# Block products of two units interleaved, four plain units first, half of the output projection plain

## The chip, the cores and the metric

The kernel runs on one core of a Trainium2 chip. The metric is device time in microseconds (us) of one execution, the median of three runs. Beside it stands one profiled execution, whose trace gives every duration below.

## What is computed

One layer of a decoder trunk for 512 tokens of width 2048, all in float32. The input is normalised, one matrix of 2048 x 8192 maps it to eight groups of 1024 columns (q, f, i, g of a gated linear recurrence with 8 heads; q, k, v, g of a dilated ALiBi attention with 16 heads), both mixers run, and one matrix of 2048 x 2048 maps their joined outputs back onto the residual stream:

```python
h = rms_norm(x, norm_gain[layer])
z = jnp.einsum('bsd,de->bse', h, w_in[layer])
q_h, f_h, i_h, g_h, q_a, k_a, v_a, g_a = jnp.split(z, split_points, axis=-1)
y_h = hgrn2_mixer(q_h, f_h, i_h, lb_all[layer], hgrn_gnorm[layer]) * silu(g_h)
y_a = dilated_attention_mixer(q_a, k_a, v_a) * silu(g_a)
y = jnp.concatenate([y_h, y_a], axis=-1)
x = x + jnp.einsum('bse,ed->bsd', y, w_out[layer])
return rms_norm(x, final_gain)
```

## The kernel before, in words

**Pieces.** A float32 product is made from three fast products: each operand is cut into a high part, which ACT makes by a cast (`cut`, L107), and a low part, which DVE makes by subtracting (L108). Each pair of tiles then costs three matmuls: hi x hi, hi x lo, lo x hi. A cut weight piece is 128 x 512, and five pairs hi/lo are in flight (`piece`).

**Units.** The input projection is worked off in 32 units of 256 columns (two blocks of 128): 16 for the recurrent heads (two per head), 16 for the attention pairs (two per pair). `plain_unit` makes the first two units (PLAIN = 2) the usual way: 16 k tiles, two blocks, two halves of the tokens, three matmuls of 128x256 each, 192 in all.

**Seven products.** All other units use the Winograd form of Strassen's scheme: seven products of half size instead of eight, 168 matmuls. The sums of the input are made once: x7 in unit 0 (`x7`, L162), x5 and x6 in unit 1, x3 after it. The sums of weights are made while loading: a raw tile is loaded by an SP queue transfer (`begin`), and a transfer on POOL's queue adds the next block to it in place (`grow`, accumulating). Tile A is loaded once and grown three times (for products 7, 6, 4), B is loaded and grown once (1, 5), D and C are loaded (2, 3). In SBUF A has two tiles, B one, and C and D share one (`W_BUFS`, L567). The order within a unit is 7, 1, 2, 6, 3, 5, 4 (`ORDER`, L55). Each product has two steps; at each step `cut_w` cuts the pieces four steps ahead, and once a tile is cut for the last time in its present state it issues the next `begin` or `grow`.

**Banks.** Products 1, 6 and 5 accumulate in one PSUM bank (a), 7 and 4 in one of two (c), 2 and 3 open a third (t). After product 1, ACT copies the bank (L709), and only then may product 6 go on adding into it; so too after product 6 (L713) and product 5.

**Mixers.** Their work is put into a calendar of slots (`at_slot`, `tick`): one slot per step, whose functions are written ahead of that step's matmuls. The recurrent head begins with `work_f` and `work_q` at the end of its first unit and `work_v`, `work_g` at the end of its second; an attention pair with `work_aq`, `work_ak`, then `work_av`, `work_ag`. Finished outputs go to DRAM (`y_dram`).

**Output projection.** It is done in two halves of 1024 columns (u = 0, 1), each by seven products of 8 k tiles, two row blocks and three matmuls of 128x512 (`o_product`), 336 matmuls a half. Its left operand, y and the sums of y's blocks, is staged back from DRAM and cut: `y_71` during the last unit, `y_2653` and `y_4` in slots of the projection's first products. Raw weights come by `o_begin`/`o_grow`, cuts by `o_cut`, five pieces ahead. `evacuate` adds each product into the residual tiles, `squares` and `finish` do the last norm. `open_out2` loads the final gain and multiplies it into the first half's tiles on GpSimd (`gained`, L876).

Of the kernel before, what the change touches and what calls it, by code (L numbers as in the profile page):

```python
# [33 lines left out]
def _units():  # L34
    out = []
    for h in range(HEADS_H):
        out.append((("f", h, 1024 + P * h), ("q", h, P * h)))
        out.append((("v", h, 2048 + P * h), ("g", h, 3072 + P * h)))
    for j in range(PAIRS):
        out.append((("aq", j, 4096 + P * j), ("ak", j, 5120 + P * j)))  # L40
        out.append((("av", j, 6144 + P * j), ("ag", j, 7168 + P * j)))
    return out
# [3 lines left out]
PLAIN = 2  # L46
# [13 lines left out]
NEXT = {("A", 7): 6, ("A", 6): 4, ("B", 1): 5}  # L60
# [3 lines left out]
def tile_kernel(ctx: ExitStack, tc: tile.TileContext, x, xT, w_in, w_out, gain, lbl, gnorm, fgain,  # L64
# [45 lines left out]
    def x_tiles(m):  # L110

        return [tuple(xp.tile([P, 4, HS], F32R, tag=f"X{m}{p}{t}", name=f"X{m}{p}{t}") for p in "hl")
                for t in range(2)]
# [15 lines left out]
    def load_x(upto):  # L129
        while len(xts) < min(upto, KT):  # L130
            k = len(xts)
            xt = st.tile([P, S], F32, tag="xt", name=f"xt_{k}", bufs=9)
            nc.sync.dma_start(xt, xT[k * P:(k + 1) * P, :])
            xts.append(xt)
# [19 lines left out]
    def square_x(k):  # L154
        if k == 0:
            A.activation(acc, xts[k], AF.Square)
        else:
            sq = st.tile([P, S], F32, tag="sq", name=f"xsq_{k}", bufs=3)
# [181 lines left out]
    def work_q(h, q):  # L340
        V.scalar_tensor_tensor(q, q, 0.5, cs["rrow"], op0=ALU.mult, op1=ALU.mult)
        H[h]["q"] = q
        at_slot(2, silu, q, H["hg"], "t", 1, f"q{h}")

    def work_g(h, g):
        V.scalar_tensor_tensor(g, g, 0.5, cs["rrow"], op0=ALU.mult, op1=ALU.mult)
        H[h]["g"] = g
        at_slot(3, silu, g, H["hg"], "t", 1, f"g{h}")

    def work_v(h, src):  # L350
        hg, aux, o = H["hg"], H[h], {}
# [90 lines left out]

    def work_aq(j, q):
        V.scalar_tensor_tensor(q, q, -0.125, cs["rrow"], op0=ALU.mult, op1=ALU.mult)
        H["aq"] = q

    def work_ak(j, k):
        V.tensor_mul(k, k, cs["rrow"])
        q = H["aq"]
# [26 lines left out]
        def scores(i, qb):  # L476
# [6 lines left out]
            p = pr[i, qb] = at.tile([P, S], F32, tag="pr", name=f"pr_{n}", bufs=4)  # L483
# [27 lines left out]

        d = H["wait"] = 4 if j == 0 else 0
        at_slot(d + 1, bias, 0)
        at_slot(d + 1, parts, 0)
        at_slot(d + 2, parts, 1)
        for n in range(8):
            at_slot(d + 4 + 2 * n, scores, n // 4, n % 4)
            at_slot(d + 4 + 2 * n + 3, turn, n // 4, n % 4)
        at_slot(d + 11, bias, 1)

    def work_ag(j, g):
        V.scalar_tensor_tensor(g, g, 0.5, cs["rrow"], op0=ALU.mult, op1=ALU.mult)
        H["pair", j]["g"] = g
        at_slot(2 + H["wait"], lambda: silu(g, H["at"], "pr", 4, f"ag{j}"))

    def work_av(j, src):
# [19 lines left out]
        at_slot(9 + H["wait"], values)  # L546
# [20 lines left out]
    W_BUFS = {"A": 2, "B": 1, "C": 1}  # L567
# [11 lines left out]
    def plain_weights(u):  # L579

        r = {}
        for n, (blk, tag) in enumerate(((W11, "A"), (W12, "B"), (W21, "A"), (W22, "C"))):
# [27 lines left out]
    def plain_unit(u):  # L610
# [3 lines left out]
        for k in range(KT):  # L614
            kg, kb = divmod(k, 4)
            t = kg % 2
            if u == 0:
# [18 lines left out]
            if kb == 2 and kg == 3 and u + 1 < PLAIN:  # L636
                cut_plain(u + 1, 0)
# [9 lines left out]
        if u == 0:  # L647
# [3 lines left out]
            close(st_cm)  # L651
            open_hg()
        for n, (kind, i, _) in enumerate(blocks):
# [3 lines left out]
            WORK[kind](i, z)  # L657


    steps = [(u, s, t) for u in range(PLAIN, len(UNITS)) for s in range(7) for t in range(2)]  # L660
    cuts = []

    def cut_w(upto):
        while len(cuts) < min(upto, len(steps)):
            u, s, t = steps[len(cuts)]
            m, b, _, _ = ORDER[s]
# [3 lines left out]
            if t == 1:  # L670
                if m == 2:
                    begin(u, "C")
                if (b, m) in NEXT:
                    grow(u, b, NEXT[b, m])
                elif u + 1 < len(UNITS) and b == "B":
                    begin(u + 1, "B")
                if u + 1 < len(UNITS):
                    if m == 3:
                        begin(u + 1, "D")
                    if m == 6:  # L680
                        begin(u + 1, "A")
                        grow(u + 1, "A", 7)
# [3 lines left out]
    def product(u, s, i0):  # L686

        m, b, tag, opens = ORDER[s]
        if opens:
            banks[tag] = bank(tag, f"{tag}{m}_{u}")  # L690
        ps = banks[tag][:, :HS]
        for t in range(2):
# [4 lines left out]
            for kb in range(4):  # L697
# [4 lines left out]
                T.matmul(ps, lo[:, c], xh[:, kb], start=False, stop=en, skip_group_check=not opens)  # L702
        (k0, i, _), (k1, _, _) = UNITS[u]
# [12 lines left out]
        elif m == 5:  # L716
            for c in (slice(HS, S), slice(0, HS)):
                V.scalar_tensor_tensor(z["z1"][:, c], ps, -1.0, z["z1"][:, c], op0=ALU.mult, op1=ALU.subtract)
        else:
            V.tensor_add(z["z0"][:, HS:], ps, z["z0"][:, HS:])  # L720
            for n, (kind, _, _) in enumerate(UNITS[u]):
                WORK[kind](i, z[f"z{n}"])
# [4 lines left out]
    Y = {}  # L727

    def staged(k, tag, pool, bufs):
        s = pool.tile([P, S], F32, tag=tag, name=f"ys_{k}_{now[0]}", bufs=bufs)  # L730
# [7 lines left out]
    def y_cut(m, kb, src):  # L738
        cut(*y_parts(m, kb), src)

    def y_71(kb):
        for m in (7, 1):
            if m not in Y:
                Y[m] = x_tiles(m)
        h = staged(kb, "zA", zp, 2)
        V.tensor_sub(h[:, HS:], h[:, :HS], h[:, HS:])
        y_cut(7, kb, h[:, HS:])
        y_cut(1, kb, h[:, :HS])

    def y_2653(kb):  # L750

        for m in (2, 6, 3, 5):
# [312 lines left out]
```

## Time and profile before

| what | value |
|---|---|
| median of three runs | 1075.66 us (1072.43 to 1079.53) |
| profiled execution | 1074.24 us |
| its span, first to last instruction | 1072.5 us |
| TensorE busy, mean granted clock | 954.5 us (89%), 0.959 |
| DVE busy | 768.2 us (72%) |
| ACT busy | 584.6 us (55%) |
| POOL busy | 245.5 us (23%) |

PE is TensorE, DVE VectorE, ACT ScalarE, POOL GpSimd, SP the engine whose queue issues most transfers. Busy time of PE counts overlapping matmuls once, and its idle time is what is left of a stretch. The granted clock is 1 at 2.4 GHz and 0.5 at 1.2 GHz.

### The profile page before, as it was taken

What the parts mean: (1) busy time and instruction counts of PE and PEld (TensorE: products, weight loads), DVE (VectorE), ACT (ScalarE), POOL (GpSimd) and SP (SyncE); (2) the same over time, 40 slices, a digit from 0 to 9 for tenths busy, and PEclk for the clock granted to TensorE, in tenths of its full rate; (3) what the DMA queues carried; (4) which work ended last, traced back from release to release, by engine and by line L of the source; (5) the groups of instructions that cost most, each with busy time, mean ns of one, the idle gap of its engine ahead of it and who ended that gap; (6) DMA issues with size and microseconds to landing.
All of it is one profiled execution on the core that took longest, in us unless ns stands there. A gap on an engine that the chain in (4) does not pass through costs nothing.

```text
span 1072.5 us, 18864 instructions
## 1 busy us (share of the span) xinstructions
PE 954.5 (89%) x7000; PEld 889.5 (83%) x7000; DVE 768.2 (72%) x1536; ACT 584.6 (55%) x1250; POOL 245.5 (23%) x259
## 2 busy tenths in 40 slices
PE   5768989899999999899999999999999686898795
PEld 4667889899989999899999899989898654677684
DVE  7899667675858576677877686867767677465756
ACT  6643645464545555466666565656666464354345
POOL 3512121222312121212232222222222210202500
PEclk9899999999999999999999999999999888989898
DMA  7225877777777777777777777777787989969644
GB/s 260 61 59 118 173 172 192 172 178 168 167 172 179 175 181 187 171 189 175 182 176 184 167 158 171 179 176 173 166 182 194 251 219 320 265 171 224 178 109 158
DMA packets 59581, 191.70 MB, mean 179 GB/s; under 512 B 6688, under 2 KB 6720, under 8 KB 59488
## 3 DMA queue, kind: packets, MB, share of 16 engines
q0 software_dynamic: 22624, 81.95, 42.8%
q1 hardware_dynamic: 36576, 108.02, 29.9%
q8 instruction: 55, 0.90, 0.3%
q10 hardware_dynamic: 288, 0.52, 0.1%
q14 instruction: 38, 0.31, 0.1%
HBM read 182.08 MB, written 8.39 MB: 178 GB/s over the span
## 4 chain that ended last, share of the span: by engine, by line
PE 37%; DMA 27%; DVE 19%; ACT 9%; issue 6%; POOL 1%; SPq 0%; ACTq 0%; DVEq 0%; POOLq 0%
DMA wA<-w_in_dram 11%; DMA wC<-w_in_dram 7%; DVE lo L108 5%; PE a L700 4%; PE a L701 3%; PE a L702 3%; ACT hi L107 2%; PE t L700 2%; PE t L702 2%; PE t L701 2%; PE ao L539 2%; DMA wB<-w_in_dram 2%; DMA r<-x_dram 2%; DMA ys<-yd 2%; PE oa L954 2%
## 5 line engine op out<-in xcount | busy, mean ns | idle before, releaser
L108 DVE TENSOR_TENSOR lo<-wA,hi 128x512 fp32r<-128x512 f32 x180 | 127.7, 712 | 106.9 <-ACT hi L107 101.7
L107 ACT CAST hi<-wA 128x512 fp32r<-128x512 f32 x180 | 109.7, 618 | 147.0 <-DMA wA<-w_in_dram 78.1
L576 POOL DMA_DIRECT2D wA<-w_in_dram x90 | 79.2, 932 | 429.6 <-DVE lo L108 297.6
L107 ACT CAST hi<-wB 128x512 fp32r<-128x512 f32 x120 | 73.0, 618 | 43.2 <-PE a L701 20.2
L700 PE MATMUL a<-X6h,hi 128*128 128x256 f32 x240 | 73.1, 305 | 20.2 <-ACT f L709 15.7
L108 DVE TENSOR_TENSOR lo<-wB,hi 128x512 fp32r<-128x512 f32 x120 | 86.0, 730 | 0.3
L108 DVE TENSOR_TENSOR lo<-wC,hi 128x512 fp32r<-128x512 f32 x60 | 45.0, 770 | 56.2 <-ACT hi L107 55.8
L700 PE MATMUL a<-X5h,hi 128*128 128x256 f32 x240 | 70.0, 292 | 4.5 <-ACT v L713 4.2
L700 PE MATMUL t<-X3h,hi 128*128 128x256 f32 x240 | 70.1, 292 | 3.1 <-DVE v L711 1.5
L107 ACT CAST hi<-wC 128x512 fp32r<-128x512 f32 x60 | 35.7, 617 | 64.4 <-DMA wC<-w_in_dram 62.2
L700 PE MATMUL t<-X2h,hi 128*128 128x256 f32 x240 | 70.7, 295 | 0.0
L702 PE MATMUL a<-X6h,lo 128*128 128x256 f32 x240 | 70.6, 294 | 0.0
L701 PE MATMUL a<-X6l,hi 128*128 128x256 f32 x240 | 70.6, 294 | 0.0
L700 PE MATMUL a<-X1h,hi 128*128 128x256 f32 x240 | 70.4, 293 | 0.0
L702 PE MATMUL c<-X7h,lo 128*128 128x256 f32 x240 | 68.1, 284 | 2.1 <-DVE lo L108 2.1
L700 PE MATMUL c<-X4h,hi 128*128 128x256 f32 x240 | 68.9, 287 | 0.0
L701 PE MATMUL a<-X1l,hi 128*128 128x256 f32 x240 | 68.6, 286 | 0.0
L700 PE MATMUL c<-X7h,hi 128*128 128x256 f32 x240 | 68.6, 286 | 0.0
L702 PE MATMUL a<-X1h,lo 128*128 128x256 f32 x240 | 68.5, 285 | 0.0
L702 PE MATMUL t<-X2h,lo 128*128 128x256 f32 x240 | 68.3, 285 | 0.0
L701 PE MATMUL t<-X2l,hi 128*128 128x256 f32 x240 | 68.3, 284 | 0.0
L702 PE MATMUL t<-X3h,lo 128*128 128x256 f32 x240 | 67.9, 283 | 0.2 <-DVE lo L108 0.2
(369 smaller groups left out, 3452.4 us busy)
## 6 DMA issues: line engine op xcount, KB each, us to landing
wA<-w_in_dram POOLq DMA_DIRECT2D x90, 512.0 KB, 5.8
wA<-w_in_dram SPq DMA_DIRECT2D x30, 512.0 KB, 3.9
wB<-w_in_dram SPq DMA_DIRECT2D x30, 512.0 KB, 4.4
wD<-w_in_dram SPq DMA_DIRECT2D x30, 512.0 KB, 3.7
wB<-w_in_dram POOLq DMA_DIRECT2D x30, 512.0 KB, 8.6
wC<-w_in_dram SPq DMA_DIRECT2D x30, 512.0 KB, 5.8
oA<-w_out_dram POOLq DMA_DIRECT2D x24, 512.0 KB, 8.4
ys<-yd SPq DMA_DIRECT2D x32, 256.0 KB, 5.4
```

What stands on the lines that cost most here:

```text
L107: A.copy(hi, src)
L108: V.tensor_sub(lo, src, hi.bitcast(F32))
L539: T.matmul(o_ps[64 * i:64 * i + 64, kb * P:], pair["v"][:, kb, 64 * i:64 * i + 64], pt[:, c0:c0 + w], start=kb == 0, stop=kb == 3)
L576: nc.gpsimd.dma_start(raws[u, b], in_tile(u, GROW[b, m]), accum_op=ALU.add)
L700: T.matmul(ps, hi[:, c], xh[:, kb], start=st_, stop=False, skip_group_check=not opens)
L701: T.matmul(ps, hi[:, c], xl[:, kb], start=False, stop=False, skip_group_check=not opens)
L702: T.matmul(ps, lo[:, c], xh[:, kb], start=False, stop=en, skip_group_check=not opens)
L954: T.matmul(ps, xh[:, tok], lo, start=False, stop=en, skip_group_check=not opens)
```

## The change

Four units are plain (PLAIN = 4), and x7 is made in unit 1, x5 and x6 in units 1 and 2. The first head's g and v are made in unit 0, before its q and f. In the other units the blocks are exchanged (z1, the block that is ready after product 5, is now the one needed first), and product 4 is done after product 7 of the next unit. W11 is no longer read a second time for product 6: DVE adds the loaded tile B to A (`add_w11`). C and D have two tiles. The last two cuts of a plain unit are followed by the first two of the products (`cut_w(2)`).

The first half of the output projection (columns 0 to 1023) is made plainly by `o_plain`: y's two halves (kh: recurrent, attention), two column blocks, 8 k tiles, four row blocks, three matmuls of 128x512, 384 in all. Its y pieces are cut by `y_hgrn` (during the last unit) and `y_attn`; `y_sums` makes the sums for the seven products of the other half in slots of the plain half.

```diff
-PLAIN = 2
+PLAIN = 4
-ORDER = [(7, "A", "c", True), (1, "B", "a", True), (2, "D", "t", True), (6, "A", "a", False),
-         (3, "C", "t", True), (5, "B", "a", False), (4, "A", "c", False)]
+PRODUCT = {7: ("A", "c", True), 1: ("B", "a", True), 2: ("D", "t", True), 6: ("A", "a", False),
+           3: ("C", "t", True), 5: ("B", "a", False), 4: ("A", "c", False)}
-GROW = {("A", 7): W22, ("A", 6): W11, ("A", 4): W21, ("B", 5): W12}
+GROW = {("A", 7): W22, ("A", 4): W21, ("B", 5): W12}
...
-            p = pr[i, qb] = at.tile([P, S], F32, tag="pr", name=f"pr_{n}", bufs=4)
+            p = pr[i, qb] = at.tile([P, S], F32, tag="pr", name=f"pr_{n}", bufs=3)
...
-    W_BUFS = {"A": 2, "B": 1, "C": 1}
+    W_BUFS = {"A": 2, "B": 1, "C": 2}
...
-                    if i < KH:
-                        x7(i)
...
+                else:
+                    cut_w(2)
...
+    order = []
+    for u in range(PLAIN, len(UNITS) + 1):
+        for m in (1, 7, 2, 6, 3, 5) if u == PLAIN else (7, -4, 1, 2, 6, 3, 5):
+            v = u - 1 if m < 0 else u
+            if PLAIN <= v < len(UNITS):
+                order.append((v, abs(m)))
+    def add_w11(raw_a, raw_b):
+        for t in range(2):
+            c = slice(512 * t, 512 * t + 512)
+            V.tensor_add(raw_a[:, c], raw_a[:, c], raw_b[:, c])
...
+            if m == (7 if u == PLAIN else 1):
+                add_w11(raws[u, "A"], raws[u, "B"])
+                grow(u, "B", 5)
+                begin(u, "C")
+            elif m == 6:
+                grow(u, "A", 4)
+            if u + 1 < len(UNITS):
+                if m == 5:
                     begin(u + 1, "B")
+                elif m == 2:
+                    begin(u + 1, "D")
+            if m == 4 and u + 2 < len(UNITS) or u == PLAIN and m == 7:
+                v = u + 1 if m == 7 else u + 2
+                begin(v, "A")
+                grow(v, "A", 7)
...
+    def y_sums(kb):
+
+        y_tiles((7, 3), (5, 5), (6, 6), (3, 7))
+        h, a = staged(kb, O["w2"], "yh"), staged(KH + kb, O["w2"], "ya")
         a11, a21, a12, a22 = h[:, :HS], h[:, HS:], a[:, :HS], a[:, HS:]
+        V.tensor_sub(a11, a11, a21)
+        cut(*y_parts(7, kb), a11)
         V.tensor_sub(a21, a22, a21)
+        V.scalar_tensor_tensor(a22, a11, -1.0, a22, op0=ALU.mult, op1=ALU.subtract)
+        cut(*y_parts(6, kb), a22)
+        V.scalar_tensor_tensor(a12, a12, -1.0, a22, op0=ALU.mult, op1=ALU.subtract)
+        cut(*y_parts(3, kb), a12)
+        cut(*y_parts(5, kb), a21)
...
+    def o_plain(kh, n, i0):
+
+        tags = ("a", "c", "c", "t")
+        ob = [mixer_bank(f"op_{sb}") if kh and n else bank(tags[sb], f"op_{kh}_{n}_{sb}") for sb in range(NSB)]
+        for kb in range(KH):
+            for sb, ps in enumerate(ob):
+                if sb % 2 == 0:
+                    tick()
+                if sb == 1:
+                    o_cut(i0 + kb + 4)
+                hi, lo = ocuts[i0 + kb]
+                xh, xl = y_parts(((1, 21), (2, 4))[kh][sb // 2], kb)
+                tok = slice(sb % 2 * P, sb % 2 * P + P)
+                T.matmul(ps, xh[:, tok], hi, start=kb == 0, stop=False)
+                T.matmul(ps, xl[:, tok], hi, start=False, stop=False)
+                T.matmul(ps, xh[:, tok], lo, start=False, stop=kb == KH - 1)
+        for sb, ps in enumerate(ob):
+            r = O["R"][0, sb // 2, n, sb % 2]
+            V.tensor_add(r, ps, r)
+            if kh:
+                squares(0, sb // 2, n, sb % 2)
...
     at_slot(12, open_out)
+    for kb in range(KH):
+        at_slot(14 + 2 * kb, y_attn, kb)
+        at_slot(32 + 3 * kb, y_sums, kb)
+        if kb < 4:
+            at_slot(30 + 2 * kb, o_begin, "A", kb)
+            at_slot(31 + 2 * kb, o_begin, "B", kb)
+            at_slot(31 + 2 * kb, o_grow, "A", 7, kb)
```

## Rows read from the trace of the kernel before

**Rows 1.** The page, busy tenths of PE in 40 equal slices.
```profile
PE   5768989899999999899999999999999686898795
```

**Rows 2.** Busy time by stage: stretch, its length, PE, PEld, DVE, ACT, POOL, clock, DMA.
```profile
0.00:50.00 50.00, 30.69 (x189) 28.09 (x190) 40.18 (x69) 32.22 (x70) 24.79 (x25) 0.93 0.52 171
50.00:87.50 37.50, 28.65 (x216) 27.36 (x215) 34.22 (x57) 14.53 (x24) 6.17 (x8) 0.91 0.30 75
87.50:143.50 56.00, 49.08 (x390) 46.61 (x390) 44.60 (x82) 28.01 (x55) 10.67 (x13) 0.97 0.67 153
143.50:442.50 299.00, 278.11 (x2348) 273.67 (x2348) 210.60 (x427) 155.06 (x318) 66.25 (x72) 0.98 0.75 175
442.50:848.00 405.50, 390.29 (x3157) 374.78 (x3156) 297.59 (x639) 251.33 (x568) 98.10 (x100) 0.99 0.78 179
848.00:1062.00 214.00, 177.67 (x711) 139.03 (x709) 136.21 (x253) 100.02 (x210) 38.47 (x41) 0.90 0.78 209
1062.00:1072.50 10.50, 0.00 (x0) 0.00 (x0) 4.80 (x13) 3.39 (x6) 1.10 (x2) 0.59 0.53 201
```

**Rows 3.** Timeline of PE around one stall: start, duration, instruction, idle before.
```profile
353.45 0.28 PE L701 MATMUL t<-X2l,hi 128*128 128x256 f32 x1
353.57 0.28 PE L702 MATMUL t<-X2h,lo 128*128 128x256 f32 x1
356.10 0.39 PE L700 MATMUL a<-X6h,hi 128*128 128x256 f32 x1 [2.25 <-ACT f L709]
...
357.83 0.41 PE L700 MATMUL a<-X6h,hi 128*128 128x256 f32 x1
```

**Rows 4.** Timeline of ACT around the same stall.
```profile
355.16 0.62 ACT L107 CAST hi<-wC 128x512 fp32r<-128x512 f32 x1 [4.29 <-DMA wC<-w_in_dram]
355.68 0.37 ACT L709 COPY f<-a 128x256 f32<-128x256 f32 x1
```

**Rows 5.** Waits of PE, 143.5 to 442.5: total, times, longest.
```profile
PE a L700 <- ACT f L709: 15.2, 6, 3.2
PE a L700 <- ACT v L713: 4.2, 5, 1.7
```

**Rows 6.** Waits of ACT, 143.5 to 442.5.
```profile
ACT hi L107 <- DMA wC<-w_in_dram: 35.5, 12, 5.1
ACT hi L107 <- DMA wA<-w_in_dram: 34.7, 11, 4.5
```

**Rows 7.** Waits of PE in the output projection, 848 to 1062.
```profile
PE ot L952 <- ACT hi_o L107: 11.8, 2, 7.0
PE ot L954 <- DVE lo_o L108: 9.6, 4, 6.0
PE oc L952 <- DVE av L720: 5.5, 1, 5.5
```

**Rows 8.** Groups of DVE in unit 0: busy us, mean ns of one, idle before.
```profile
L168 DVE SCALAR_TENSOR_TENSOR X7l<-d,gain_sb,X7h 128x256 fp32r<-128x256 f32 x8 | 4.8, 605 | 0.0
```

**Rows 9.** Timeline of DVE in unit 0.
```profile
35.52 0.47 DVE L152 SCALAR_TENSOR_TENSOR X2l<-xt,gain_sb,X2h 128x256 fp32r<-128x256 f32 x1
35.91 0.47 DVE L152 SCALAR_TENSOR_TENSOR X4l<-xt,gain_sb,X4h 128x256 fp32r<-128x256 f32 x1
36.31 1.50 DVE L152 SCALAR_TENSOR_TENSOR X2l<-xt,gain_sb,X2h 128x256 fp32r<-128x256 f32 x1
```

**Rows 10.** Groups of DVE in the second plain unit (one sum of x5).
```profile
L178 DVE TENSOR_TENSOR d<-X4h,X3h 128x1024 f32<-128x1024 f32 x2 | 2.4, 1209 | 0.6 <-PE rrow_ps L262 0.6
```

**Rows 11.** Timeline of PE in the output projection.
```profile
971.06 0.39 PE L954 MATMUL oc<-lo_o,X7h 128*128 128x512 f32 x1
971.29 0.39 PE L952 MATMUL oc<-hi_o,X7h 128*128 128x512 f32 x1
```

**Rows 12.** The page, DMA issues: engine, count, KB each, median us to landing.
```profile
wB<-w_in_dram POOLq DMA_DIRECT2D x30, 512.0 KB, 8.6
wC<-w_in_dram SPq DMA_DIRECT2D x30, 512.0 KB, 5.8
...
ys<-yd SPq DMA_DIRECT2D x32, 256.0 KB, 5.4
```

**Rows 13.** Timeline of DVE after the final gain has landed.
```profile
1001.62 12.05 DVE L108 TENSOR_TENSOR lo_o<-oD,hi_o 128x512 fp32r<-128x512 f32 x4 [2.89 <-ACT hi_o L107]
```

More of the change, by code (lines that the diff above doesn't have):

```diff
@@ L108, in cut, with x_tiles @@
         V.tensor_sub(lo, src, hi.bitcast(F32))
-    def x_tiles(m):
-        return [tuple(xp.tile([P, 4, HS], F32R, tag=f"X{m}{p}{t}", name=f"X{m}{p}{t}") for p in "hl")
+    def x_tiles(m, of=None):
+        return [tuple(xp.tile([P, 4, HS], F32R, tag=f"X{of or m}{p}{t}", name=f"X{m}{p}{t}") for p in "hl")
                 for t in range(2)]
@@ L718, in product, with staged @@
                 V.scalar_tensor_tensor(z["z1"][:, c], ps, -1.0, z["z1"][:, c], op0=ALU.mult, op1=ALU.subtract)
+            WORK[k1](i, z["z1"])
         else:
             V.tensor_add(z["z0"][:, HS:], ps, z["z0"][:, HS:])
-            for n, (kind, _, _) in enumerate(UNITS[u]):
-                WORK[kind](i, z[f"z{n}"])
+            if u == 2 * HEADS_H:
+                close(H["cm"])
+                close(H["dcm"])
+                open_at()
+            WORK[k0](i, z["z0"])
     Y = {}
-    def staged(k, tag, pool, bufs):
-        s = pool.tile([P, S], F32, tag=tag, name=f"ys_{k}_{now[0]}", bufs=bufs)
+    O = {}
+    def staged(k, pool, tag):
+        s = pool.tile([P, S], F32, tag=tag, name=f"ys_{k}_{now[0]}", bufs=2)
         nc.sync.dma_start(s, y_dram[k])
@@ L736, in y_parts, with y_tiles @@
         return tuple(a[:, b] for a in Y[m][t])
[L738 to L742, printed above, removed]
+    def y_tiles(*which):
+        for m, of in which:
             if m not in Y:
[L744 to L752, printed above, removed]
-            if m not in Y:
-                Y[m] = x_tiles(m)
-        h, a = staged(kb, "zB", zp, 2), staged(KH + kb, "zA", zp, 2)
+                Y[m] = x_tiles(m, of)
@@ L838, in open_out @@
         O["ssq"] = w2.tile([P, NSB, 4], F32, name="ssq")
-        for jb in range(2):
-            o_begin(0, "D", jb)
         O["R"] = {}
@@ L848, in open_out @@
                     O["R"][0, th, n, blk] = r
-        for fn in O.pop("late"):
-            fn()
-        O["late"] = None
     def open_out1():
         for i, (th, n) in enumerate(((1, 1), (0, 0), (1, 0), (0, 1))):
-            r = xp.tile([P, 2, 512], F32, tag=("X7h0", "X7l0", "X7h1", "X7l1")[i], name=f"r1_{th}_{n}")
+            r = xp.tile([P, 2, 512], F32, tag=("X3h0", "X3l0", "X3h1", "X3l1")[i], name=f"r1_{th}_{n}")
             for blk in range(2):
@@ L868, in open_out2 @@
             O["fg"].append(f)
-        O["sq"] = xp.tile([P, 2, 512], F32, tag="X1l0", name="osq")
-        for key in O["R"]:
-            if key[0] == 0:
-                gained(*key)
-    def gained(u, th, n, blk):
-        r = O["R"][u, th, n, blk]
-        G.tensor_mul(r, r, O["fg"][u][:, 512 * n:512 * n + 512])
+        for u, th, n, blk in O["R"]:
+            if u == 0:
+                r = O["R"][u, th, n, blk]
+                G.tensor_mul(r, r, O["fg"][0][:, 512 * n:512 * n + 512])
     def squares(u, th, n, blk):
```

296 lines of the change are left out of this document (142 added, 154 removed).

## The prediction

> **What bounds the kernel now.** I read the page's slices first: TensorE is at 98% or more in the middle and clearly lower in about the first five slices and the last ten [rows 1]. The table by stage then puts borders where the work changes [rows 2]: the first plain unit (0 to 50 us), the second (50 to 87.5), the first two units made by seven products (to 143.5), twelve more units of the recurrent heads (to 442.5), sixteen units of the attention heads (to 848), the output projection (to 1062), and 10.5 us without a matmul. PE busy minus the stretch is the idle time: 20.9 us in the fourth stage, 15.2 in the fifth, 36.3 in the sixth. The clock column is the second loss. A mean of 0.98 between the levels 0.5 and 1 means 4% of the time at 1.2 GHz; 0.90 means 20%.
>
> The timeline of PE gives the pitch: 0.12 us from one 128x256 matmul to the next (the 0.28 beside it is the latency of a pipelined one) [rows 3]. It also shows the typical stall: the last matmul of product 2 starts at 353.57, the first of product 6 at 356.10, and soon after it the matmuls take 0.41 instead of 0.28, that is 1.2 GHz. Product 6 adds into the bank that product 1 has filled, so it needs ACT's copy of that bank. ACT's timeline shows why the copy is late: it stands behind a cast that waited 4.29 us for the single tile wC to land, and runs right after it, at 355.68 [rows 4]. The waits of PE for this stage are nearly all of this kind: 15.2 us for product 6 and 4.2 for product 5 [rows 5], and ACT stood 35.5 us for wC and 34.7 for wA [rows 6]. So this stage is bound by TensorE plus loads that come too late for ACT's queue.
>
> **The change part by part.** *Start.* x7's 16 DVE instructions leave unit 0, where DVE was busy 40.2 of 50 us [rows 2]. Their mean there is 0.605 us [rows 8], so at most 9.7 us go; neighbours on DVE last either 0.47 or 1.50 us [rows 9], and the undisturbed ones start 0.40 apart, so 16 are worth 6.4. I take 6: unit 0 ends at 44 (bounds 40 and 50).
>
> Here the Trainium skill bears on the sum (SBUF — State Buffer, Who interferes with whom): a DVE instruction with two SBUF inputs and a GpSimd instruction that reads SBUF lock each other out for a whole instruction. By it the long ones are charged to the 15 additions of squares on GpSimd, which stay, and only 6.4 us go; by the mean it would be 9.7. The two lengths agree with the rule. It speaks against the change too: the new sums of raw weights on DVE have two SBUF inputs.
>
> Units 1 to 3 are 3 x 192 matmuls x 0.12 = 69 us, and head 0's small matmuls some 4 (in the fourth stage 278 us busy less 12 x 168 x 0.12 = 242 for the products and 6 of half rate leave 30 for six heads, at most 5 each). What DVE does beside them: the 34.2 us of the old unit 1 (its sums are 1.21 us each [rows 10]), x7 6, the cuts of two more units 16 x 0.6 = 10, head 0 some 11, together 61. That fits under 73, but not evenly: the old unit 1 took 37.5 us where its matmuls need 23. I add 8 for waits: 125. Two cuts are now made before the products begin, while x3's eight long instructions still fall there: of the 6 us by which the third stage exceeds two later units (56 against 2 x 24.9) I keep 3. So the state "28 units left" comes at 128 instead of 143.5: **15.5 us gained** (0 to 26: with 20 us of waits and the 6 kept, or none of either).
>
> *Steady units.* Product 4 of a unit moves behind product 7 of the next, D and C get two tiles, and the sum for product 6 is made on DVE from tiles that have landed instead of by a third accumulating DMA on A. C is now issued with the cut of product 1 and used by the cut of product 3, three products (some 10 us) later; it lands in 5.8 us at the median [rows 12]. B's growth has four products, A's last growth four too, a fresh A most of a unit. So ACT's waits for wC and wA should nearly go, and with them the late copies. Cost in the twelve recurrent units: 299 us, 24.9 each; 20.9 us idle, and 4% at half rate costs another 6, together 27. I let a quarter stay: **20 us gained** (0 to 27). The additions take 2 x 0.6 = 1.2 us of DVE per unit (half the length of the sum in [rows 10]); DVE is busy 210.6 of 299 us, so at 24.9 less 1.7 per unit it would be at about 81%: hidden beside PE. What is queued behind an addition on DVE is the next lo; the two cuts of lead (two products, near 7 us) cover it. On the queues each unit issues seven 512 KB transfers instead of eight, three of them on POOL instead of four. What is late next: the small matmuls of the mixers.
>
> The attention units have 15.2 us idle in 405.5, in good part waits for softmax rows, and these get one buffer less (three in place of four). The additions bring 19 us of DVE work. **5 us gained**; bounds -19 (all additions in the open) and +12.
>
> *Output projection.* Half of it becomes plain: 384 matmuls of 512 columns for 336. The pitch is 0.23 [rows 11], so 48 more cost 11 us. Against that: of the 214 us the 672 matmuls need 153, the rest of the last attention pair some 5 (in the fifth stage 390 busy less 16 x 168 x 0.12 = 323 leave 8 a pair); some 56 are lost, 36 idle and the rest at half rate. The waits name them [rows 7]: cuts whose raw tile or y summand is late (11.8 and 9.6), the copy behind y's staging (5.5). In the plain half a cut feeds four row blocks, 12 matmuls, 2.7 us, and the lead of four cuts is 11 us; the staged y tiles land in 5.4 [rows 12], and the summands for the other half are made one per three slots, 4 us, with at most 3 us of DVE each. The first quarter needs only the recurrent heads' y, so the last attention pair ends under it. I keep 5 at the border, 8 in the plain half and 12 in the other. Most of that last is one known event: multiplications on GpSimd stretch four lo's to 12 us [rows 13], and they stay. 56 - 25 - 11 = **20 us gained** (-11 to 30). The last 10.5 us stay.
>
> The other edits (blocks exchanged within a unit, moved slots, squares of the first half into PSUM, y tiles in other buffers) change no count, and I cost them at nothing: PE works beside them. Where a slot is moved badly the price is a stall like that before product 6, 2.4 us a time [rows 3]. The plain half also needs no accumulating transfers: 16 tiles of 512 KB where the old half took 32.
>
> Sum: 15.5 + 20 + 5 + 20 = 60.5. The profiled execution took 1074.2 us (span 1072.5 and 1.7 around it); the median of the runs is 1075.7. So 1013.7 by the profile's execution, **1015** by the median.
>
> **Rivals.** (a) The loads are no longer late but the products are no faster: ACT also waits for PE to free pieces, and DVE's lo for ACT's hi, so the chain hi, lo, matmul could set the pace. For it: the same ACT queue serves casts, copies and mixers. Against it: ACT was busy 155 of 299 us [rows 2]. Steady units then give nothing, start and output 35.5: 1040. (b) The plain half keeps the old losses, because staging, 64 casts and the sums meet the attention tail on the same queues: the output stage costs 11 more; 15.5 + 20 + 5 - 11 = 29.5 gained: 1046. Against it is the lead of four cuts. (c) All the waits that I kept go as well: 26 + 27 + 12 + 30 = 95 gained, 981. (d) Slower: the addition waits for B and for A's accumulating DMA, and DVE stands with it in its own order; B has one tile, is asked for only when the cut of product 5 is done and must be there three products later. If it comes late, every unit stops PE by w. Start and output give 35.5, so from w = 1.3 us in 28 units on the change is a loss; at w = 2, two thirds of what ACT waits for wC per unit now (35.5 / 12), 1096. For it: POOL's queue waits in order for landings (8.6 us at the median for wB grown there [rows 12]). Against it: SP's queue loses its waits for wC.
>
> **How the numbers follow.** Forecast 0.55, (a) 0.17, (b) 0.12, (c) 0.08, (d) 0.08. The forecast's own bounds and (a) and (b) make 988 to 1050 as the range; outside lie (c), (d) and sums of two rivals. About 1% (10.8 us) is what a measurement of this kernel can tell from no change. Faster by more: the first four cases, 0.92, less 0.05 for (a) and (b) together: 0.87. Within: 0.05. Slower: 0.08.
>
> **What would show it.** Right: unit 0 ends near 44 and the first seven-product unit begins near 125; ACT's waits for wC and wA shrink from 70 us to under 20 in the recurrent units and PE's wait for product 6's copy from 15 to under 4; a recurrent unit takes 23.2 us; output matmuls begin near 810 and run at 0.23 through the plain half; the clock is over 0.97 there. Wrong: units still at 24.9 with ACT waits moved to another tile; DVE above 90% with lo late; the plain half longer than 105 us; a PE wait per unit behind the additions.

## The result and the profile after

The changed kernel takes 1010.97 us, the median of four runs (1009.90 to 1011.71). The kernel before took 1074.66 us on the same chip (1072.43 to 1079.53). The ratio is 0.9401, with a 95% interval of 0.9366 to 0.9435. The profiled execution is the one of 1009.90 us, its span 1008.1 us, the mean granted clock 0.981.

The table by stage of the changed kernel has the columns of [rows 2]: stretch, its length, PE, PEld, DVE, ACT, POOL, clock, DMA share and GB/s. The borders are the same events: the end of unit 0, 28 units left, the first attention unit, the output projection's plain half, its half by seven products, the tail.

```profile
0.00:43.50 43.50, 30.59 (x193) 28.59 (x194) 35.09 (x58) 29.12 (x64) 26.17 (x25) 0.92 0.57 209
43.50:123.40 79.90, 77.36 (x648) 75.79 (x649) 73.58 (x133) 37.85 (x70) 15.08 (x12) 1.00 0.35 96
123.40:401.50 278.10, 271.36 (x2348) 268.78 (x2346) 219.39 (x447) 159.15 (x321) 53.21 (x59) 1.00 0.66 162
401.50:798.60 397.10, 388.25 (x3155) 373.16 (x3155) 318.03 (x675) 260.49 (x579) 78.33 (x81) 1.00 0.65 161
798.60:911.20 112.60, 98.99 (x423) 78.17 (x423) 67.22 (x153) 45.88 (x109) 4.79 (x5) 0.94 0.63 199
911.20:997.20 86.00, 79.33 (x337) 63.77 (x335) 61.19 (x88) 40.28 (x76) 20.29 (x20) 0.96 0.52 141
997.20:1008.10 10.90, 0.00 (x0) 0.00 (x0) 4.82 (x14) 3.34 (x6) 1.10 (x2) 0.67 0.51 196
```

Against [rows 2]: 28 units are left at 123.4 instead of 143.5 (20.1 us gained), twelve recurrent units take 278.1 instead of 299.0 (20.9), sixteen attention units 397.1 instead of 405.5 (8.4), the output projection 198.6 instead of 214.0 (15.4), and the tail 0.4 more. That is 64.4 us in all. The trace has 2348 matmuls in the recurrent units, as before. PE's idle time there falls from 20.9 to 6.7 us and its clock rises from 0.98 to 1.00.

Waits of the changed kernel in the recurrent units, 123.4 to 401.5 (total, times, longest), beside [rows 5] and [rows 6]:

```profile
DVE wA L682 <- DMA wB<-w_in_dram: 13.9, 11, 2.3
...
PE vp_h L276 <- DVE v L744: 5.8, 4, 1.6
...
ACT hi L107 <- DMA wB<-w_in_dram: 4.5, 4, 1.2
...
ACT hi L107 <- DMA wA<-w_in_dram: 3.8, 2, 2.6
```

ACT's 35.5 us for wC are off the list, the 34.7 for wA have become 3.8, and PE no longer waits for the copies behind products 1 and 6. What is new is the first line: DVE stands at the additions (L682) for tile B. e3, e5 and e12 look for what that costs.

The plain half shows its losses in PE's timeline. Each pair is the last matmul of a quarter and the first of the next:

```profile
828.49 0.39 PE L957 MATMUL op<-lo_o,X1h 128*128 128x512 f32 x1
831.37 0.50 PE L955 MATMUL op<-hi_o,X21h 128*128 128x512 f32 x1 [2.50 <-DVE r L960]
...
851.33 0.39 PE L957 MATMUL op<-lo_o,X21h 128*128 128x512 f32 x1
856.03 0.77 PE L955 MATMUL op<-hi_o,X2h 128*128 128x512 f32 x1 [4.31 <-DVE r L960]
...
879.99 0.39 PE L957 MATMUL op<-lo_o,X4h 128*128 128x512 f32 x1
886.22 0.79 PE L955 MATMUL op<-hi_o,X2h 128*128 128x512 f32 x1 [5.85 <-ACT osq L898]
```

A quarter ends, and the next one needs the same banks: they come free only when DVE has added them to the residual (L960). The last quarter takes other banks, into which the squares of the third one are written, and waits until ACT is through with these (L898). DVE's timeline shows why the additions themselves are late:

```profile
830.63 0.69 DVE L960 TENSOR_TENSOR r<-op,r 128x512 f32<-128x512 f32 x1 [2.59 <-DMA r<-x_dram]
...
853.86 0.42 DVE L108 TENSOR_TENSOR X2l<-ys,X2h 128x256 fp32r<-128x256 f32 x1 [3.44 <-ACT X2h L107]
...
855.20 1.88 DVE L960 TENSOR_TENSOR r<-op,r 128x512 f32<-128x512 f32 x3
```

At the first border an addition waits for its part of the residual to land, at the second the additions stand behind a lo of y that waits for its hi, whose tile was late. After the two longer idle times the first matmul takes 0.77 and 0.79 us, twice the 0.39 before them: the granted clock is 0.50 there (854.1 to 861.0 and 884.8 to 891.7), that is 1.2 GHz.

### The profile page after: what moved, and what is told of

Read it like the earlier page. It is cut to its first block, busy times and chain, and to the rows that moved or that the text cites. A ratio compares the mean times of both kernels' runs of the same rounds, so it can differ in the third digit from the quotient of the medians.

```text
span 1008.1 us, 18861 instructions
## 1 busy us (share of the span) xinstructions
PE 945.9 (94%) x7096; PEld 888.3 (88%) x7096; DVE 779.3 (77%) x1564; ACT 576.1 (57%) x1218; POOL 199.0 (20%) x203
## 4 chain that ended last, share of the span: by engine, by line
PE 62%; DVE 14%; DMA 10%; issue 8%; ACT 3%; POOL 2%; SPq 0%; DVEq 0%; POOLq 0%; ACTq 0%
PE a L725 6%; PE a L727 6%; PE a L726 6%; PE t L725 4%; PE t L727 4%; PE t L726 4%; DMA ys<-yd 3%; PE c L726 3%; PE c L725 3%; PE c L727 3%; DVE lo L108 3%; DMA wB<-w_in_dram 3%; PE ao L547 2%; PE op L955 2%; DVE lo_o L108 2%
## 5 line engine op out<-in xcount | busy, mean ns | idle before, releaser
L107 ACT CAST hi<-wA 128x512 fp32r<-128x512 f32 x168 | 103.3, 619 | 93.9 <-PE a L726 52.6
L108 DVE TENSOR_TENSOR lo<-wA,hi 128x512 fp32r<-128x512 f32 x168 | 114.7, 690 | 18.4 <-ACT hi L107 17.6
L584 POOL DMA_DIRECT2D wA<-w_in_dram x56 | 49.5, 883 | 141.3 <-DVE lo L108 124.8
L682 DVE TENSOR_TENSOR wA<-wA,wB 128x512 f32<-128x512 f32 x56 | 39.4, 713 | 44.8 <-DMA wB<-w_in_dram 44.8
L725 PE MATMUL a<-X1h,hi 128*128 128x256 f32 x224 | 65.1, 291 | 0.0
L725 PE MATMUL a<-X6h,hi 128*128 128x256 f32 x224 | 64.8, 289 | 0.1
L725 PE MATMUL t<-X2h,hi 128*128 128x256 f32 x224 | 64.1, 286 | 0.0
L726 PE MATMUL t<-X3l,hi 128*128 128x256 f32 x224 | 63.9, 285 | 0.0
L727 PE MATMUL a<-X6h,lo 128*128 128x256 f32 x224 | 63.4, 283 | 0.0
L726 PE MATMUL a<-X5l,hi 128*128 128x256 f32 x224 | 63.3, 283 | 0.0
```

The lines of the kernel that those rows point to most:

```text
L107: A.copy(hi, src)
L108: V.tensor_sub(lo, src, hi.bitcast(F32))
L584: nc.gpsimd.dma_start(raws[u, b], in_tile(u, GROW[b, m]), accum_op=ALU.add)
L682: V.tensor_add(raw_a[:, c], raw_a[:, c], raw_b[:, c])
L725: T.matmul(ps, hi[:, c], xh[:, kb], start=st_, stop=False, skip_group_check=not opens)
L726: T.matmul(ps, hi[:, c], xl[:, kb], start=False, stop=False, skip_group_check=not opens)
```

## The experiments

All are edits of the changed kernel, but for e10. A recurrent unit is the mean over eight, from the first matmul of product 7 in unit 6 to that in unit 14; an attention unit likewise from 20 to 28. Halves of the output run from first matmul to first matmul, the last to its last matmul. The runs come from several chips (medians of before 1067.5 to 1076.8), so ratios are compared.

| run | median us | ratio, 95% interval | recurrent unit | attention unit | plain half | other half |
|---|---|---|---|---|---|---|
| before | 1074.66 | 1 | 25.02 | 24.95 | none | none |
| changed | 1010.97 | 0.9401 (0.9366 to 0.9435) | 23.18 | 24.34 | 112.5 | 85.6 |
| e11, changed again | 1012.42 | 0.9405 (0.9350 to 0.9461) | 23.17 | 24.41 | 113.3 | 87.3 |
| e1, one C/D tile | 1057.18 | 0.9821 (0.9767 to 0.9875) | 24.68 | 27.21 | 111.9 | 84.5 |
| e2, no interleaving | 1025.91 | 0.9520 (0.9458 to 0.9582) | 23.88 | 24.75 | 113.0 | 84.3 |
| e3, sum by transfer | 1000.41 | 0.9305 (0.9259 to 0.9352) | 22.84 | 23.96 | 112.2 | 85.0 |
| e4, two plain units | 1024.73 | 0.9521 (0.9477 to 0.9566) | 23.56 | 24.28 | 113.0 | 86.4 |
| e5, addition later | 1008.12 | 0.9437 (0.9407 to 0.9467) | 23.17 | 24.33 | 113.1 | 83.6 |
| e6, other banks | 996.37 | 0.9349 (0.9304 to 0.9394) | 23.18 | 24.39 | 102.7 | 84.6 |
| e7, gain spread | 1011.23 | 0.9468 (0.9441 to 0.9495) | 23.18 | 24.25 | 114.2 | 83.4 |
| e8, e3 + e6 + more | 983.57 | 0.9215 (0.9183 to 0.9248) | 22.50 | 23.96 | 101.2 | 84.0 |
| e9, old output | 1037.13 | 0.9642 (0.9589 to 0.9694) | 23.18 | 24.41 | none | none |
| e10, before + tile | 1055.57 | 0.9810 (0.9757 to 0.9864) | 23.83 | 24.93 | none | none |
| e12, additions behind lo | 994.39 | 0.9267 (0.9207 to 0.9326) | 22.64 | 23.79 | 112.0 | 87.6 |

**e1: C and D share one tile again.**

```diff
-    W_BUFS = {"A": 2, "B": 1, "C": 2}
+    W_BUFS = {"A": 2, "B": 1, "C": 1}
...
-                begin(u, "C")
+            if m == 2:
+                begin(u, "C")
...
-                elif m == 2:
+                elif m == 3:
                     begin(u + 1, "D")
```

(The plain units' block W12 goes to B's tile for want of the second one, and a raw tile of the output to another place.)

> The changed kernel, but C and D share one tile again: C is loaded after the cut of product 2, D of the next unit after the cut of product 3. Theory (the seven-product units were held up by loads that came late for ACT's queue): the copy before product 6 is late again, a recurrent unit goes from 23.2 back to 24.4 or more, 1030 to 1045 us. Rival (the exchanged order of the products made the gain, the second tile is a detail): at most 1018 us.

It takes 1057.18 us, 46 more than the changed kernel. Waits of ACT in e1 name the tile, in the recurrent units (125 to 395) and in the attention units (415 to 790):

```profile
ACT hi L107 <- DMA wC<-w_in_dram: 33.5, 11, 5.0
...
ACT hi L107 <- DMA wC<-w_in_dram: 53.1, 12, 6.1
```

The 33.5 us answer to the 35.5 of [rows 6]. So the wait for wC comes back with the shared tile, and with it 1.5 us a recurrent unit. It stops PE at another place than the theory said. The copy before product 6 is not on PE's list of the recurrent units; what is there is the start of product 3, which needs C's own pieces:

```profile
PE t L726 <- DVE g L738: 9.6, 4, 3.4
```

The weight loads of the same four starts wait 10.3 us for ACT's hi. The attention units become 2.3 us slower than before the change, which I had not expected: there the wait is longer still. Why the shared tile hurts more in the new order than it did in the old was not settled.

**e2: no interleaving.**

```diff
-        for m in (1, 7, 2, 6, 3, 5) if u == PLAIN else (7, -4, 1, 2, 6, 3, 5):
+        for m in (1, 7, 2, 6, 3, 5, 4) if u == PLAIN else (7, 1, 2, 6, 3, 5, 4):
```

> The changed kernel with product 4 back at the end of its own unit; everything else stays. Theory: A's last growth has three products of lead instead of four, which is still more than its landing takes, so 1010 to 1020 us. Rival (the interleaving of two units is what made the units faster): recurrent units back at 24 or more, 1030 us or more.

It takes 1025.91 us: 15 more, 0.7 a recurrent unit and 0.4 an attention unit. That is more than the theory gave and less than the rival. ACT waits for wA again, in the two stretches of e1:

```profile
ACT hi L107 <- DMA wA<-w_in_dram: 18.9, 5, 4.4
...
ACT hi L107 <- DMA wA<-w_in_dram: 15.6, 6, 3.0
```

So the two edits answer to the two waits of [rows 6]: the tile to wC, the interleaving to part of wA.

**e10: the kernel before with the second tile alone.**

```diff
-    W_BUFS = {"A": 2, "B": 1, "C": 1}
+    W_BUFS = {"A": 2, "B": 1, "C": 2}
...
-                if m == 2:
+                if m == 1:
                     begin(u, "C")
...
-                    if m == 3:
+                    if m == 2:
                         begin(u + 1, "D")
```

> The kernel before with one part of the change alone: D and C have a tile each, C is begun with the cut of product 1 and the next D with the cut of product 2 (each one product earlier), and softmax rows have three buffers. No interleaving, two plain units, three accumulating transfers on A. Theory (the second tile is most of what the steady units gain: without it the changed kernel lost 1.5 us a recurrent unit, without interleaving 0.7): the waits of ACT for wC nearly go, those for wA stay, a recurrent unit falls from 25.0 to 24.2 us or less, the whole is 1045 to 1062 us, ratio 0.972 to 0.988. Rival (the tile pays only together with the interleaving and the addition on DVE, which keep A from being late): ACT waits for wA instead of wC, units 24.7 or longer, ratio 0.990 or more.

It takes 1055.57 us, ratio 0.981. Waits of ACT in e10, 143.5 to 430:

```profile
ACT hi L107 <- DMA wA<-w_in_dram: 55.6, 18, 4.5
ACT hi L107 <- DMA wB<-w_in_dram: 15.4, 6, 2.9
```

A recurrent unit falls by 1.19 us of the 1.84 that the whole change gives it. wC is off the list, and ACT waits for wA (55.6 us, 34.7 before) and wB instead: 71.0 us in all, as much as the 70.2 before. Yet PE's wait for the copy behind product 1 (15.2 us in [rows 5]) is gone, and that for the copy behind product 6 is 8.7 us (4.2 before). So ACT's wait cost PE by what stood behind it, not by its length. An attention unit gains nothing (24.93). The tile is the larger part of the gain in the recurrent units even alone; in the attention units it needs the rest of the change.

**e4: two plain units instead of four.**

```diff
-PLAIN = 4
+PLAIN = 2
...
-        if u == 2:
-            at_slot(6, x5, 1)
-            at_slot(10, x6, 1)
+            at_slot(14, x5, 1)
+            at_slot(15, x6, 1)
```

> The changed kernel with two plain units instead of four; the sums x5, x6 of both halves then fall into unit 1. Theory (the four plain units cover the sums of x and the first head's work on DVE): the first seven-product units stall as before, 20 us lost at the start less 2 x 0.9 us for the dearer plain units, so 1022 to 1032 us. Rival (moving x7 out of unit 0 made the gain at the start, and plain units only cost more matmuls): 1005 to 1013 us.

It takes 1024.73 us, as the theory said, and unit 16 begins 13.9 us later (412.3 against 398.4). Unit 6 begins 9.9 us later (176.5 against 166.6), so some 10 of the 20 us gained at the start come from making units 2 and 3 plain. The other 4 are lost in the recurrent units behind it (23.56 us each against 23.18), for a reason that is open. The page's slices of PE in e4 show where the first units wait, in the fourth and sixth slice:

```profile
PE   5896989999999999989999999999999898989795
```

**e6: the plain half's second column block on other banks.** The squares of the first half go into the bank that was just read.

```diff
-        ob = [mixer_bank(f"op_{sb}") if kh and n else bank(tags[sb], f"op_{kh}_{n}_{sb}") for sb in range(NSB)]
+        ob = [mixer_bank(f"op_{kh}_{sb}") if n else bank(tags[sb], f"op_{kh}_{n}_{sb}") for sb in range(NSB)]
...
-                squares(0, sb // 2, n, sb % 2)
+                squares(0, sb // 2, n, sb % 2, ps)
```

> The changed kernel, but in the plain half the two column blocks use two different sets of PSUM banks in turn, and the squares of the first half go into the bank just read. Theory (the plain half lost its time where a quarter waits for the evacuation of the one before, 13.3 us of PE waits and the clock at 0.94 after them): plain half 112.6 to 95 us, 992 to 1000 us in all. Rival (the late y pieces then wait in their stead): 1004 us or more.

The plain half takes 102.7 instead of 112.5 us. Waits of PE in it (804.5 to 907.2 of this run, the two largest):

```profile
PE op L958 <- DVE lo_o L108: 4.5, 2, 3.2
PE op L956 <- ACT hi_o L107: 0.7, 1, 0.7
```

The waits for L960 and for the squares (6.8 and 6.5 us in the changed kernel) are gone. So PE had to pay for the late additions because of the reuse of banks. Cuts that come late behind the sums of y take part of their place, so the half does not reach the 95 us of the theory.

**e9: both halves of the output by seven products again,** with the functions of the kernel before (the diff is that part of the change, reversed).

```diff
-    def o_plain(kh, n, i0):
...
+    osteps = [(u, s, kb) for u in range(2) for s in range(7) for kb in range(KH)]
...
+    for u in range(2):
+        for s in range(7):
...
+            o_product(u, s, i0)
             i0 += KH
```

> The changed kernel with the output projection of the kernel before: both halves by seven products. Its first four plain units, interleaved block products and separate tiles for D and C stay. Theory (the plain half gains what the stages say, 15 us of the 64): the output stage takes 210 to 215 us again, the units keep their 23.2 and 24.3, and the whole is 1022 to 1030 us, ratio 0.950 to 0.958. Rival (the seven-product output is slow mainly because it inherits late transfers and a late mixer from the units, so with the new units it would be as fast as the plain half): output stage under 205 us, ratio 0.947 or less.

It takes 1037.13 us, 25 more than the changed kernel beside it (e11), and is slower than either theory said. The output takes 220.6 us from its first matmul to its last, where e11 takes 200.6, and it begins 7.7 us later. Waits of ACT in e9's output (807 to 1028):

```profile
ACT hi_o L107 <- DMA oC<-w_out_dram: 22.1, 3, 15.4
ACT X2h L107 <- DMA ys<-yd: 17.4, 5, 12.3
```

PE stands 21.5 us for three such cuts, the longest 10.3; in [rows 7] the longest is 7.0. So the plain half is worth 25 us beside these units, more than the 15.4 by which the stage shortened, because the old output joined to the new units is slower than it was with the old ones. That its losses were inherited from the old units is refuted.

**e7: the multiplications by the final gain in two groups,** to keep them from the cuts ([rows 13]).

```diff
+            if m in (6, 3):
+                gained((6, 3).index(m))
```

> The changed kernel, but the eight multiplications by the final gain on GpSimd come four after product 6 and four after product 3 of the projection instead of all after product 1. Theory (DVE and GpSimd lock each other out, and the lead of five cuts bears four of them but not eight): the 6.3 us wait goes, 1003 to 1007 us. Rival (the same lock, only elsewhere): 1009 to 1013 us.

No gain: 0.9468. The timeline of POOL in e7 tells why:

```profile
945.27 3.06 POOL L894 TENSOR_TENSOR r<-r,fg 128x512 f32<-128x512 f32 x2 [12.46 <-DMA fg<-fgain_dram]
...
948.86 7.43 POOL L894 TENSOR_TENSOR r<-r,fg 128x512 f32<-128x512 f32 x6
```

All eight still run in one stretch as soon as the gain has landed. Beside them DVE's timeline has four lo's in 12.08 us:

```profile
944.77 12.08 DVE L108 TENSOR_TENSOR lo_o<-oA,hi_o 128x512 fp32r<-128x512 f32 x4
```

Where the statement stands in the program did not decide where the engine runs it. The run therefore says nothing on the price of this stretch; PE still stands 4.8 us behind it.

**e3: the sum for product 6 by an accumulating transfer.**

```diff
-GROW = {("A", 7): W22, ("A", 4): W21, ("B", 5): W12}
+GROW = {("A", 7): W22, ("A", 6): W11, ("A", 4): W21, ("B", 5): W12}
...
+            if m == 7:
+                grow(u, "A", 6)
...
-                add_w11(raws[u, "A"], raws[u, "B"])
```

> The changed kernel, but W11 is read a second time and added to A by an accumulating transfer after the cut of product 7, as before, instead of by DVE. Theory (the additions are hidden beside TensorE, and with the new order the transfer has five products of lead): 1005 to 1016 us. Rival (the additions, which wait for B, hold DVE and so TensorE): under 1003 us. Second rival (the transfers themselves were too many for POOL's queue): over 1020 us.

It takes 1000.41 us, 10 less: 0.34 us a recurrent unit and 0.38 an attention unit, 28 units. So the additions on DVE were not hidden. They could cost by their length (the page's group L682: 39.4 us for 56, 713 ns each) or by DVE's stand for tile B in front of them (13.9 us above).

**e5: the addition written one product later.** The growth of B goes with it.

```diff
             if m == (7 if u == PLAIN else 1):
-                add_w11(raws[u, "A"], raws[u, "B"])
-                grow(u, "B", 5)
                 begin(u, "C")
+            elif m == 2:
+                add_w11(raws[u, "A"], raws[u, "B"])
+                grow(u, "B", 5)
```

> The changed kernel with the addition on DVE one product later (after the cut of product 2 instead of product 1, together with B's growth). The run without the addition took 1000 us. Theory (what the addition cost is its wait for B at the head of DVE's queue, 44.8 us of DVE's idle time): 999 to 1005 us. Rival (its 39 us of busy time on DVE are the cost): 1008 to 1014 us.

Nothing changes: 0.9437, units of 23.17 and 24.33. By the expectation that is a verdict for length. DVE's timeline in e5 forbids it:

```profile
213.31 0.81 DVE L682 TENSOR_TENSOR wA<-wA,wB 128x512 f32<-128x512 f32 x1 [1.90 <-DMA wB<-w_in_dram]
214.04 0.68 DVE L108 TENSOR_TENSOR lo<-wA,hi 128x512 fp32r<-128x512 f32 x1
214.65 0.68 DVE L682 TENSOR_TENSOR wA<-wA,wB 128x512 f32<-128x512 f32 x1
215.25 0.68 DVE L108 TENSOR_TENSOR lo<-wA,hi 128x512 fp32r<-128x512 f32 x1
215.85 0.74 DVE L745 SCALAR_TENSOR_TENSOR v<-a,v 128x256 f32<-128x256 f32 x2
216.51 1.28 DVE L108 TENSOR_TENSOR lo<-wB,hi 128x512 fp32r<-128x512 f32 x2
```

The same stretch of the changed kernel has the same order:

```profile
212.63 0.89 DVE L682 TENSOR_TENSOR wA<-wA,wB 128x512 f32<-128x512 f32 x1 [1.25 <-DMA wB<-w_in_dram]
213.45 1.10 DVE L108 TENSOR_TENSOR lo<-wA,hi 128x512 fp32r<-128x512 f32 x1
214.47 0.68 DVE L682 TENSOR_TENSOR wA<-wA,wB 128x512 f32<-128x512 f32 x1
215.07 0.68 DVE L108 TENSOR_TENSOR lo<-wA,hi 128x512 fp32r<-128x512 f32 x1
215.67 0.74 DVE L744 SCALAR_TENSOR_TENSOR v<-a,v 128x256 f32<-128x256 f32 x2
```

In both, the additions run ahead of the lo's of product 4 (from wA) and of product 1 (from wB), although the program writes them behind these. What waits behind the first addition is the lo of product 4, whose hi ACT had cut by 211.5 us in the changed kernel, and v, for which PE stood 5.8 us.

**e12: the additions forced behind the lo's of product 1** by a factor of one that is read from the last of them.

```diff
+        one = wp.tile([P, 1], F32, tag="one", name=f"one{now[0]}", bufs=2)
+        V.tensor_scalar(one, lo[:, 0:1].bitcast(F32), 0.0, 1.0, op0=ALU.mult, op1=ALU.add)
         for t in range(2):
             c = slice(512 * t, 512 * t + 512)
-            V.tensor_add(raw_a[:, c], raw_a[:, c], raw_b[:, c])
+            V.scalar_tensor_tensor(raw_a[:, c], raw_b[:, c], one, raw_a[:, c], op0=ALU.mult, op1=ALU.add)
```

> The changed kernel with the additions forced behind the lo of the second piece of product 1 on DVE, by a factor of one that is read from that lo (one DVE instruction more a unit, 128x1). In the changed kernel, and in the run that wrote the addition one product later, DVE's own order has each addition ahead of the lo's of product 4 and of product 1, and DVE stands there 1.2 us a unit for B to land (13.9 us in the twelve recurrent units). Theory A (that stand is what the additions cost, and the sum by transfer gains by removing it): the waits of DVE for wB go, a recurrent unit takes 22.8 to 22.95 us and an attention unit 24.0 to 24.1 instead of 23.18 and 24.34, ratio 0.929 to 0.934. Theory B (the cost is their occupancy of DVE, 1.4 us a unit, which the transfer also removes): units of 23.15 to 23.3 and 24.3 to 24.5, ratio 0.939 to 0.944.

It takes 994.39 us, ratio 0.9267 against 0.9401 and 0.9405 for the changed kernel. A recurrent unit takes 22.64 us, an attention unit 23.79, less than either theory gave. DVE's timeline of e12 at the same place:

```profile
211.22 1.28 DVE L108 TENSOR_TENSOR lo<-wA,hi 128x512 fp32r<-128x512 f32 x2
212.42 0.74 DVE L746 SCALAR_TENSOR_TENSOR v<-a,v 128x256 f32<-128x256 f32 x2
213.09 2.46 DVE L108 TENSOR_TENSOR lo<-wB,hi 128x512 fp32r<-128x512 f32 x2
215.58 0.15 DVE L681 TENSOR_SCALAR one<-lo 128x1 f32<-128x1 f32 x1
215.77 1.42 DVE L684 SCALAR_TENSOR_TENSOR wA<-wB,one,wA 128x512 f32<-128x512 f32 x2
```

v runs at 212.42 instead of 215.67, and PE's wait for it in the recurrent units falls from 5.8 to 0.9 us. DVE no longer waits for wB; ACT does (45.4 us, 4.5 in the changed kernel), and PE's list has no wait for a cut. The table by stage has the recurrent units of e12 in this row:

```profile
123.40:395.20 271.80, 267.57 (x2345) 264.19 (x2343) 224.90 (x462) 156.02 (x318) 60.09 (x58) 1.00 0.68 165
```

DVE works 5.5 us more there than in the changed kernel (224.90 against 219.39). So the additions' length in total is not the price. What is left is their place, with what it puts ahead of v: the stand and the two additions themselves, which this run does not part.

What the place is worth can't be read from the units. Of the 6.3 us by which the stretch is shorter, PE's idle time gives 2.5 (6.7 to 4.2); the rest is busy time on the same matmuls (271.36 to 267.57). That rest does not come from the additions, for it is there before the first of them. In the plain units, whose matmuls the edit leaves alone, they start 0.113 us apart in e12, at a granted clock of 1.00:

```profile
60.79 0.28 PE L654 MATMUL c<-X2l,hi_p 128*128 128x256 f32 x1
60.91 0.28 PE L655 MATMUL c<-X2h,lo_p 128*128 128x256 f32 x1
61.02 0.28 PE L653 MATMUL t<-X4h,hi_p 128*128 128x256 f32 x1
61.13 0.28 PE L654 MATMUL t<-X4l,hi_p 128*128 128x256 f32 x1
```

The changed kernel has 0.120 there, and so has every other trace of this case. In e12's recurrent units the mean pitch is 0.118 and in its attention units 0.116. With 168 matmuls that is some 0.4 of the 0.54 us by which a recurrent unit is shorter, and the whole 0.55 of an attention unit (estimates). Matmuls of 512 columns are slower in e12, 0.233 instead of 0.227. Why the pitch differs is open; beside the order of DVE, the edit adds a small tile to the pool of the weight pieces. What is left for the place of the additions is PE's idle time: 2.5 us less in the recurrent units and 2.3 in the attention units. e3 takes 2.5 and 3.3 from it.

**e8: e3, e6 and e7 together, and the recurrent head's `turn_values` a slot later.**

```diff
-        for dt, fn in ((1, carry), (2, turn_values), (4, scores), (5, turn), (8, states), (11, outputs), (14, scale),
+        for dt, fn in ((1, carry), (3, turn_values), (4, scores), (5, turn), (8, states), (11, outputs), (14, scale),
```

> The changed kernel with the sum by transfer, the two sets of banks, the spread multiplications, and the transposes of the recurrent head's values one slot later. If the parts add up: 1000 less 13 to 18, less 4 to 8, less 3 to 8, so 970 to 985 us. If they share one limit: 988 to 996 us.

It takes 983.57 us, ratio 0.9215: it beats both kernels. The gains of e3 (0.0096) and e6 (0.0052) add to 0.0148; the ratio fell by 0.0186. The rest fits the moved slot, which was not run alone: PE's wait for v is gone from the recurrent units, whose waits of PE in e8 (123.4 to 391.6) are this one line:

```profile
PE y L436 <- ACT os L431: 0.8, 1, 0.8
```

e12's ordering and e6's banks were not run together, and e12's ordering not at the usual pitch.

**e11: the changed kernel again.**

> The changed kernel again, unaltered, beside the others on this chip, as the measure for runs of a few microseconds: ratio 0.937 to 0.944 by both theories.

It takes 1012.42 us, ratio 0.9405, as expected; e9, e10 and e12 are read against it.

## Why the prediction was right, and where it was not

The forecast was 1015 us, 4 more than the result, and 60.5 us gained by the profiled execution, where the stages show 64.4. That the sum came so near is in part luck: the start and the attention units gave 8 us more than forecast, the output 4.6 less. Step by step:

**Start: 15.5 forecast, 20.1 measured.** Unit 0 ended at 43.2 (44 forecast), and the three plain units took 80.1 (81). The 3 us that I kept for x3's long instructions beside the first products did not show: PE's longest idle time between 118.1 and 214 is 0.81 us. One reading for unit 0 was wrong: 0.605 us is the mean of eight of x7's sixteen instructions, the other eight take 0.414. So at most 8.0 us could go and not 9.7, which leaves the 6 that were taken as they are.

**Recurrent units: 20 forecast, 20.9 measured.** 23.18 us a unit against 23.2 forecast, waits for wC and wA off the list or nearly. e1, e2 and e10 show that it is for the stated reason, loads that come late for ACT's queue, with the tile as the larger part: 1.19 us alone, 1.50 as the last step; the interleaving is worth 0.70 on top. (The slices of [rows 1] do not say 98%, a 9 is 90% or more; by [rows 2] PE was busy 93% of the recurrent and 96% of the attention units.) Rival (a), a chain of hi, lo and matmul that keeps its pace, is refuted.

One term in this step was wrong and hidden by the sum. I held the additions to be hidden beside PE because "the two cuts of lead cover it". Their length was right (1.4 us a unit, 1.2 forecast; DVE busy 79%, 81 forecast). But the lead counts from the program's order, and DVE ran each addition ahead of the lo's that it should have followed. That is rival (d)'s mechanism, DVE standing in its own order for B, at a smaller size: without the additions (e3) a recurrent unit is 0.34 us shorter and an attention unit 0.38, some 10 us in 28 units. With the additions pinned behind the lo's (e12) PE's idle time in these units falls by 4.8 us; the larger gain of that run is for the most part its other pitch. The quarter of the loss that I "let stay" had room for it in the recurrent units.

**Attention units: 5 forecast, 8.4 measured,** within the bounds. e3 shows 0.38 us a unit more to be had by taking the additions off DVE, 6.1 us in sixteen, so my bound of 12 for all that could be gained here was too tight: 8.4 and 6.1 are 14.5.

**Output: 20 forecast, 15.4 measured.** The half by seven products took 86.0, where 336 x 0.23 and the 12 kept make 89. The plain half took 112.6, and I had said that more than 105 would be wrong; the clock there, forecast over 0.97, was 0.94. By the measured pitch its 384 matmuls need 87 and the last attention pair some 5, which leaves 20.6 lost; I kept 13 (5 at the border, 8 in the half). The mechanism that I weighed, late cuts, was rightly small. What I missed are banks: three quarters on the same four, and the fourth on those that the squares of the third are written into, so that each begins only when DVE has added the one before. And these additions came late, since DVE stood ahead of them for the residual and for y's pieces, or was busy with y's sums. 13.6 us are named waits (6.8, 6.5 and 0.3). The clock was at half for 13.7 us; 3.3 of them fall into these waits, and the other 10.4 cost some 5 more (an estimate). No row names the last 2. e6 took 9.8 of the 20.6 back.

That the 12 us kept in the other half were "one known event" holds in part: 6.3 us of wait remain behind the multiplications on GpSimd, where DVE takes 10.93 us for four lo's that take 0.69 each alone. That agrees with the rule of the Trainium skill (SBUF — State Buffer, Who interferes with whom) by which the prediction priced such neighbours: DVE and GpSimd lock each other out of a shared pair of ports. By that rule the new additions, which have two SBUF inputs, would stretch too where GpSimd reads SBUF beside them; their median here is 0.69 us and the longest 1.52, so little of their cost can have come that way.

**Rival (b)** said that the plain half keeps the old losses. e9 puts the plain half's worth at 25 us, so it fell, although the losses that remained were larger than forecast.

## What to carry to other kernels

Read the waits of the engine that feeds the bottleneck, tile by tile: here two waits of ACT, for two raw tiles, were answered by two edits, and each comes back when its edit is undone (wA's in part). An instruction that waits for a transfer costs what stands behind it on its engine: in e10 ACT stood as long as before and the units were 1.19 us shorter. So look at its place in the engine's timeline, since the program's order may not be the engine's. Where the place matters, pin it by a dependency on data: a moved statement that the engine runs where it did before is no experiment. And before a gain is put down to an edit, compare the two traces where the edit changes nothing: e12's plain units showed that part of its gain had another source.

## What was not expected of the hardware

A third growth on A (e3) adds a transfer of 512 KB a unit and raises the DMA share of the recurrent units from 0.66 to 0.82, and yet the two growths that both kernels make landed no later: 8.3 and 6.7 us at the median in e3, 8.3 and 6.9 in the changed kernel. (The page's median for A falls from 7.1 to 6.1 because the third lands in 5.5.)

Two idle times of PE were followed by different matmuls: after 2.50 us the first took 0.50, with the granted clock at 1.00, after 4.31 us it took 0.77 at 0.50, where 0.39 is usual.

One build (e12) ran its matmuls at another pitch than the thirteen other traces, which have 0.120 us for 256 columns and 0.227 for 512: 0.113 to 0.118 and 0.233, from the plain units to the end, at the same granted clock.
